# Delta rule of a hybrid decoder layer: per-head scalings and squares as ScalarE activations, the decay's subtraction as the exponential's bias, z's product as one VectorE instruction

## The chip, the cores and the metric

The kernel runs on one core of a Trainium2 chip. A core has five engines with queues of their own: PE (TensorE, matmuls), DVE (VectorE), ACT (ScalarE), POOL (GpSimd) and SP (SyncE, which here only issues DMAs). Each engine takes its instructions strictly in the order of the built program; semaphores hold an instruction until what it needs is there. The metric is the device time of one execution in microseconds; three runs of the kernel before gave 1560.11 to 1562.34 us, median 1561.56 us.

## The reference, cut to what matters

One decoder layer over 1024 tokens of width 1024, all in float32: RMSNorm, one input projection, then two groups of heads side by side, an output projection, a SwiGLU FFN, a gated embedding and a last norm. The change touches the gated delta rule of four heads (width 128, chunks of tokens; the kernel works with chunks of 128), and there these parts:

```python
gc = cumsum(g)                                   # per chunk, log decay
decay = where(lower, exp(gc[:, None] - gc[None, :]), 0)
kk = (k * beta) @ k.T * decay                    # strict lower part + identity = a_mat
u, w = solve(a_mat, [v * beta, k * beta * exp(gc)])
v_new = u - w @ state
o = (q * exp(gc)) @ state + (q @ k.T * decay) @ v_new
state = state * exp(g_last) + (k * exp(g_last - gc)).T @ v_new
o = o * rsqrt(mean(o * o) + EPS) * norm_w * silu(z)
```

## The kernel before, in words

The layer is one program in stages. First x is normalised and transposed and the v columns of the attention group are projected. Then comes the stage that matters here, from about 118 to 520 us: 24 units of the input projection ("pj": 128 output columns each, in two halves of 512 tokens, 24 matmuls of 128x512 per half) are the filling work of PE, and the delta rule of the four heads is woven between them. Softmax attention (from about 520 us), the FFN (from about 735 us) and the rest follow.

**Order of PE.** Generators (scan, prep, inv, output and so on) and the filler are woven by `weave` (L221). It asks a planner, class `Plan` (L53), when each operand will be ready. The planner adds fixed costs per instruction, by engine and free size (`op`, L94), and whenever no step of the delta rule is ready by its clock, one more group of three projection matmuls is put on PE. So PE's order is frozen while the program is written. The orders of ACT, DVE, POOL and, in this stage, SP come from a scheduler that runs afterwards on its own cost model. A change of instruction costs or engines therefore moves instructions on every engine.

**The delta rule, per head h and group g of four chunks.** `gates` (L512) makes the cumulative decays. `prep` (L703) transposes k and q, takes their norms, loads the row of decays (egb) by DMA and builds the decay matrix dt_ (subtraction with a per-partition scalar and a mask, four VectorE instructions of 128x128, then one Exp), multiplies it into the two products kk, and sends the triangular matrix nT to DRAM. `base` (L765) inverts small blocks with some 50 VectorE instructions and sends them through DRAM; it is tile names scr_pr, scr_uq, scr_ub. `inv` (L824) assembles the inverse U with PE (px, pz, pt, then pw, pu), ACT evacuating; X and ktok are k scaled per token, by GpSimd, after pz has read X's first content. `scan` (L899) is the serial recurrence over eight chunks (pr, pS, po). `emit_out` (L936) squares and sums the output o, scales it by its inverse norm, transposes it and multiplies by z. z itself is a projection unit: `z_half` (L609) evacuates it twice on ACT (plain, and tanh of half), GpSimd forms (1 + tanh) times plain in two instructions, and SP stores it.

The stretch from prep of a head to the end of its base is called a **base stretch** below, the stretch from there to the first step of the scan an **inversion stretch**. prep of head h+1 starts only after base of head h, and base of h+1 after inv of h, so these stretches follow each other for the four heads.

**Projection banks.** In this stage a projection half waits for one of two PSUM banks (`mmt`, L280); a bank is free when ACT has evacuated the half before the last (`conv_half` L580 into xb_g, `z_half`, or f_half).

Of the kernel before, what the change touches and what calls it, by code (L numbers as in the profile page):

```python
# [8 lines left out]
F32 = mybir.dt.float32  # L9
# [10 lines left out]
P = 128  # L20
# [167 lines left out]
def hybrid_layer(ctx, tc, x, p, attn_norm_w, w_in, conv_w, a_log, dt_bias, gdn_norm_w, fox_f_bias,  # L188
# [10 lines left out]
    def bc(ap, n):  # L199
        return ap.unsqueeze(len(ap.shape)).to_broadcast(list(ap.shape) + [n])  # L200
# [289 lines left out]
    def g4(tag, name, bufs=1, dt=F32, pool=None):  # L490
        pool = pool or (gpb if tag in ("scr", "nT", "X") else gp)
        return pool.tile([P, 4, P], dt, tag=tag, name=f"{tag}_{name}", bufs=bufs)
# [14 lines left out]
    egl = const.tile([P, NT, GH], F32, name="egl")  # L507
    egt = const.tile([P, NT, GH], F32, name="egt")
    kdw = const.tile([P, NT, GH], F32, name="kdw")
    beta = const.tile([P, NT, GH], F32, name="beta")  # L510

    def gates():  # L512
# [30 lines left out]
        mm(gl[:, 0:32], tri, ggf)  # L543
        mm(gl[:, 32:64], ones, ggf)
        V.tensor_copy(gcf, gl[:, 0:32])
        V.tensor_tensor(kdwf, gl[:, 32:64], gcf, op=ALU.subtract)
        A.activation(eglf, gl[:, 32:64], AF.Exp)
        A.activation(kdwf, kdwf, AF.Exp)
# [60 lines left out]
    def z_half(h, hf, ps):  # L609
        st = f(st1.tile([P, HALF], F32R, tag="fsh", name=f"zst{h}{hf}"))  # L610
        sp = f(st1.tile([P, HALF], F32R, tag="fsl", name=f"zsp{h}{hf}"))
        A.activation(sp, ps, AF.Copy)
        A.activation(st, ps, AF.Tanh, scale=0.5)
        G.tensor_tensor(st, st, sp, op=ALU.mult)
        G.tensor_tensor(st, st, sp, op=ALU.add)
        SY.dma_start(zs_d[h, :, hf * HALF:(hf + 1) * HALF], st)
        z_done[h] += 1

# [84 lines left out]
    def prep(h, g):  # L703
# [30 lines left out]
                                  ap=[[0, P], [GH * P, 4], [1, P]]))  # L734
        yield from ready(egb)
        dt_ = g4("scr", f"dt{nm}", 4)
        for j in range(4):
            V.scalar_tensor_tensor(dt_[:, j, :], egb[:, j, :], gc[:, t0 + j, h:h + 1], mbias,
                                   op0=ALU.subtract, op1=ALU.add)
        A.activation(egb, egb, AF.Exp)  # L740
        A.activation(dt_, dt_, AF.Exp)
        yield from ready(sm, dt_, slots=[SA])
        nT = nTs[h, g] = g4("nT", nm, 4)
        qkT = qkTs[h, g] = g4("qkT", nm, 2 * home(h)[1], pool=home(h)[0])
# [79 lines left out]
    def inv(h, g):  # L824
        nm = f"{h}_{g}"
        nT = nTs[h, g]
        kq, vT = kqv[h]
        tsl = slice(4 * g, 4 * g + 4)
        ktok, sm = ktoks[h, g], sms[h, g]
        U = g4("U", nm, 2)  # L830
        SY.dma_start(U, img(u_d[h], g))
        yield from ready(U)
        T = g4("X", f"T{nm}", 4)
        V.transpose(T.rearrange("p a b -> p (a b)"), U.rearrange("p a b -> p (a b)"))
        yield from ready(T, nT, slots=[SA])
        px = gpt(f"px5_{nm}")
        for j in range(4):
            mm(px[:, j, :], nT[:, j, :], T[:, j, :])
        X = g4("X", f"X{nm}", 4)
        A.activation(X, px, AF.Copy)  # L840
        yield from ready(X, slots=[SA])
        pz = gpt(f"pz5_{nm}")
        for j in range(4):
            mm(pz[:, j, :], X[:, j, :], U[:, j, :])
        V.copy_predicated(U, mask.unsqueeze(1).to_broadcast([P, 4, P]), pz)
        G.tensor_tensor(X, ktok, bc(egt[:, tsl, h], P), op=ALU.mult)
        G.tensor_tensor(ktok, ktok, bc(sm[:, 3], P), op=ALU.mult)
        yield from ready(U, slots=[SA])
        lo, hi = slice(0, 64), slice(64, P)
        pt = gpt(f"pt6_{nm}")  # L850
        for j in range(4):
            tr(pt[lo, j, lo], U[lo, j, lo], ident[lo, lo])
        A.activation(T[lo, :, lo], pt[lo, :, lo], AF.Copy)
        yield from ready(T, slots=[SA])
        px = gpt(f"px6_{nm}")
        for j in range(4):
            mm(px[hi, j, lo], nT[lo, j, hi], T[lo, j, lo])
        A.activation(T[hi, :, lo], px[hi, :, lo], AF.Copy)
        yield from ready(T, slots=[SA])
        pz = gpt(f"pz6_{nm}")  # L860
        for j in range(4):
            mm(pz[lo, j, hi], T[hi, j, lo], U[hi, j, hi])
        V.tensor_copy(U[lo, :, hi], pz[lo, :, hi])
        yield from ready(U, X, slots=[SA])
        pw = gpt(f"pw_{nm}")
        for j in range(4):
            mm(pw[:, j, :], X[:, j, :], U[:, j, :])
        A.activation(kq[:, tsl, 0], pw, AF.Copy, scale=-1.0)
        pu = gpt(f"pu_{nm}")
        for j in range(4):  # L870
            mm(pu[:, j, :], U[:, j, :], vT[:, 4 * g + j, :])
        V.tensor_tensor(vT[:, tsl], pu, bc(sm[:, 0], P), op=ALU.mult)
        yield from ready(kq, vT)
        left[h] -= 1
# [61 lines left out]
    def emit_out(h, g, o, sm):  # L936
        nm = f"{h}_{g}"
        sq = g4("osc", f"sqo{nm}", 2)
        G.tensor_tensor(sq, o, o, op=ALU.mult)
        so = small.tile([P, 4], F32, tag="so", name=f"so{nm}")  # L940
        V.tensor_reduce(so, sq, axis=AX.X, op=ALU.add)
        V.tensor_tensor(so, so, sm[:, 4], op=ALU.mult)
        V.tensor_tensor(so, so, sm[:, 4], op=ALU.mult)
        V.tensor_scalar(so, so, 1.0 / P, EPS, op0=ALU.mult, op1=ALU.add)
        ro = rsqrt(small, so, 4, f"o{nm}")
        V.tensor_tensor(ro, ro, sm[:, 4], op=ALU.mult)
        G.tensor_tensor(o, o, bc(ro, P), op=ALU.mult)
        while z_done[h] <= g:
            yield 0.5
        zt = g4("osc", f"zt{nm}", 2)  # L950
# [801 lines left out]
```

## Time and profile before

| | |
|---|---|
| runs | 1560.11, 1561.56, 1562.34 us (median 1561.56) |
| profiled execution | 1558.22 us, its span on the core 1556.5 us |
| mean granted TensorE clock | 0.972 of full speed |
| PE busy | 1467.6 us (94%), 7258 matmuls |
| DVE busy | 963.7 us (62%), 1989 instructions |
| ACT busy | 584.8 us (38%), 1211 instructions |
| POOL busy | 443.3 us (28%), 392 instructions |

Busy times are sums over the span. A matmul's end is modelled, so the distance from one start to the next tells more than its length. "PEclk" is the granted clock, 1.00 being 2.4 GHz and 0.50 being 1.2 GHz; a value between is a mean over the stretch. In a row such as `X_X<-ktok,egt ... x8 | 9.7, 1217 | 31.1 <-PE pz L154 20.5` the engine was busy 9.7 us with eight instructions of 1217 ns on average and sat idle for 31.1 us ahead of them, 20.5 us of it until PE's pz. Every operation goes through one helper, so the line is always L154 and the tiles tell operations apart.

### The profile page before, as it was taken

How to read it: one execution, taken by the hardware profiler on the slowest of the kernel's cores; microseconds unless marked ns; L12 is line 12 of the kernel's file. 1: busy time of each engine (PE TensorE's matmuls, PEld its weight loads, DVE VectorE, ACT ScalarE, POOL GpSimd, SP SyncE). 2: the span in 40 equal slices, each digit the busy share in tenths (PEclk: the TensorE clock that was granted, in tenths of full speed). 3: DMA queues.
4: the chain of work that ended last, by engine and by line, in shares of the span. 5: the costliest groups of instructions: out<-in, count | busy, mean ns of one | idle time of the engine just before them, and what ended most of it. 6: DMA issues, size and time to landing. Idle time of an engine off the chain costs nothing.

```text
span 1556.5 us, 20281 instructions
## 1 busy us (share of the span) xinstructions
PE 1467.6 (94%) x7258; PEld 1212.5 (78%) x7258; DVE 963.7 (62%) x1989; ACT 584.8 (38%) x1211; POOL 443.3 (28%) x392
## 2 busy tenths in 40 slices
PE   7999797989999899999689999999998999999997
PEld 6987686868787678887568888888887788888886
DVE  6569878796743367758955555555555442426555
ACT  5354433342333567755523323332322220214322
POOL 3023244344553465644422222322220000000000
PEclk9999898999999989999889999999999999999999
DMA  7322323234457876654122222222224832312022
GB/s 222 127 75 62 83 55 91 75 88 118 122 159 224 259 190 162 174 162 157 41 82 81 82 81 82 81 81 82 82 68 146 298 102 73 119 34 84 31 99 85
DMA packets 189701, 175.93 MB, mean 113 GB/s; under 512 B 30864, under 2 KB 147136, under 8 KB 189600
## 3 DMA queue, kind: packets, MB, share of 16 engines
q1 hardware_dynamic: 189200, 174.06, 38.1%
q8 instruction: 57, 0.93, 0.3%
q0 software_dynamic: 400, 0.57, 0.2%
q14 instruction: 44, 0.36, 0.1%
HBM read 122.53 MB, written 52.07 MB: 112 GB/s over the span
## 4 chain that ended last, share of the span: by engine, by line
PE 66%; DVE 18%; DMA 7%; ACT 3%; issue 2%; SPq 2%; POOL 1%; ACTq 0%; DVEq 0%; POOLq 0%
PE dn L154 15%; PE gC L154 8%; PE gD L154 7%; PE gA L154 7%; PE ppg L154 6%; PE pj L154 5%; PE gB L154 4%; DVE scr_pr L154 3%; DVE y_g L154 3%; PE v L154 2%; PE wog L154 2%; SPq L154 2%; DVE scr_uq L154 2%; PE po L154 2%; PE lg L154 1%
## 5 line engine op out<-in xcount | busy, mean ns | idle before, releaser
L154 PE MATMUL pj<-xna,wh_u 128*128 128x512 f32 x384 | 161.1, 420 | 9.5 <-ACT xb_g L154 8.5
L154 PE MATMUL pj<-xna,wl_u 128*128 128x512 f32 x384 | 152.9, 398 | 0.0
L154 PE MATMUL pj<-xnb,wh_u 128*128 128x512 f32 x384 | 152.7, 398 | 0.0
L154 ACT ACTIVATE whP<-fraw 128x512 fp32r<-128x512 f32 x110 | 68.5, 629 | 203.6 <-issue 101.1
L154 DVE TENSOR_TENSOR hr<-hr,dn 128x512 f32<-128x512 f32 x64 | 43.9, 687 | 114.5 <-PE dn L154 114.2
L154 POOL TENSOR_TENSOR s<-fraw 128x512 f32<-128x512 f32 x22 | 29.0, 1317 | 290.6 <-DMA fraw<-in_w_gate_up_dram 289.3
L154 PE MATMUL gD<-hb_T,whP 128*128 128x512 f32 x352 | 111.2, 397 | 0.0
L154 PE MATMUL gA<-hb_B,whP 128*128 128x512 f32 x352 | 111.1, 397 | 0.0
L154 POOL TENSOR_TENSOR wl_u<-wr_u,wh_u 128x512 fp32r<-128x512 f32 x48 | 70.1, 1481 | 116.0 <-ACT wh_u L154 80.9
L154 DVE TENSOR_TENSOR wlP<-fraw,whP 128x512 fp32r<-128x512 f32 x110 | 78.8, 720 | 29.4 <-ACT whP L154 29.4
L154 DVE TENSOR_TENSOR wlP<-s,whP 128x512 fp32r<-128x512 f32 x44 | 49.1, 1119 | 75.1 <-ACT whP L154 75.1
L154 PEld LDWEIGHTS pj<-xna,wh_u 128*128 128x128 f32 x384 | 74.0, 193 | 25.2 <-ACT xb_g L154 10.0
L154 PE MATMUL dn<-dh,al 128*128 128x512 f32 x224 | 89.7, 400 | 2.7 <-DVE al L154 2.7
L154 POOL TENSOR_TENSOR p<-p,rc 128x384 f32<-128x384 f32 (+3 forms) x64 | 72.6, 1146 | 63.4 <-DVE rc L154 45.3
L154 PE MATMUL dn<-dh,ah 128*128 128x512 f32 x224 | 89.4, 399 | 1.3 <-ACT ah L154 1.3
L154 PE MATMUL dn<-dl,ah 128*128 128x512 f32 x224 | 89.4, 399 | 0.5 <-DVE dl L154 0.5
L154 PEld LDWEIGHTS pj<-xna,wl_u 128*128 128x128 f32 x384 | 73.7, 192 | 16.4
L154 PEld LDWEIGHTS pj<-xnb,wh_u 128*128 128x128 f32 x384 | 74.1, 193 | 12.7
L154 PE MATMUL ppg<-dhp,pn 128*128 128x512 f32 (+1 forms) x272 | 81.8, 382 | 0.0
L154 PE MATMUL dn<-dn,ah 128*128 128x512 f32 x256 | 79.4, 391 | 0.0
L154 PEld LDWEIGHTS gA<-hb_B,whP 128*128 128x128 f32 x352 | 66.7, 190 | 15.9
L154 PEld LDWEIGHTS gD<-hb_T,whP 128*128 128x128 f32 x352 | 66.8, 190 | 15.8
(326 smaller groups left out, 3781.9 us busy)
## 6 DMA issues: line engine op xcount, KB each, us to landing
fraw<-in_w_gate_up_dram SPq DMA_DIRECT2D x44, 512.0 KB, 4.3
wr_u<-in_w_in_dram SPq DMA_DIRECT2D x24, 512.0 KB, 4.0
hb<-qk_d SPq DMA_DIRECT2D x24, 512.0 KB, 8.5
act_d<-th SPq DMA_DIRECT2D x44, 256.0 KB, 3.6
draw<-in_w_down_dram SPq DMA_DIRECT2D x22, 512.0 KB, 4.7
ar<-act_d SPq DMA_DIRECT2D x24, 384.0 KB, 3.3
v_d<-vs SPq DMA_DIRECT2D x16, 256.0 KB, 3.7
qk_d<-fsh SPq DMA_DIRECT2D x16, 256.0 KB, 3.5
```

Of the source, the lines that this page charges most:

```text
L154: r = f(*a, **kw)
```

## The change

- In `gates` a negated copy ngc of the cumulative decays is made once.
- In `prep` the four subtractions per group become one VectorE addition of the mask (128x512), and the subtraction becomes the bias of Exp, which is now four activations of 128x128.
- In `inv` X and ktok are scaled by eight ACT activations of 128x128 with a scale per partition, in place of two GpSimd instructions of 128x512.
- In `emit_out` the squares and their sums are four ACT activations with an accumulator (GpSimd's product and VectorE's reduction go), and the scaling by the inverse norm is four ACT activations (GpSimd's product goes).
- In `z_half` one VectorE instruction on 128x512 replaces GpSimd's two.

There are eight groups (four heads, two groups each) and eight halves of z.

```diff
@@ -507,6 +507,7 @@
     egl = const.tile([P, NT, GH], F32, name="egl")
     egt = const.tile([P, NT, GH], F32, name="egt")
     kdw = const.tile([P, NT, GH], F32, name="kdw")
+    ngc = const.tile([P, NT, GH], F32, name="ngc")
     beta = const.tile([P, NT, GH], F32, name="beta")
 
     def gates():
@@ -543,6 +544,7 @@
         mm(gl[:, 0:32], tri, ggf)
         mm(gl[:, 32:64], ones, ggf)
         V.tensor_copy(gcf, gl[:, 0:32])
+        V.tensor_scalar(ngc.rearrange("p t h -> p (t h)"), gl[:, 0:32], -1.0, None, op0=ALU.mult)
         V.tensor_tensor(kdwf, gl[:, 32:64], gcf, op=ALU.subtract)
         A.activation(eglf, gl[:, 32:64], AF.Exp)
         A.activation(kdwf, kdwf, AF.Exp)
@@ -611,8 +613,7 @@
         sp = f(st1.tile([P, HALF], F32R, tag="fsl", name=f"zsp{h}{hf}"))
         A.activation(sp, ps, AF.Copy)
         A.activation(st, ps, AF.Tanh, scale=0.5)
-        G.tensor_tensor(st, st, sp, op=ALU.mult)
-        G.tensor_tensor(st, st, sp, op=ALU.add)
+        V.scalar_tensor_tensor(st, st, 1.0, sp, op0=ALU.add, op1=ALU.mult)
         SY.dma_start(zs_d[h, :, hf * HALF:(hf + 1) * HALF], st)
         z_done[h] += 1
 
@@ -734,11 +735,10 @@
                                   ap=[[0, P], [GH * P, 4], [1, P]]))
         yield from ready(egb)
         dt_ = g4("scr", f"dt{nm}", 4)
+        V.tensor_tensor(dt_, egb, mbias.unsqueeze(1).to_broadcast([P, 4, P]), op=ALU.add)
+        A.activation(egb, egb, AF.Exp)
         for j in range(4):
-            V.scalar_tensor_tensor(dt_[:, j, :], egb[:, j, :], gc[:, t0 + j, h:h + 1], mbias,
-                                   op0=ALU.subtract, op1=ALU.add)
-        A.activation(egb, egb, AF.Exp)
-        A.activation(dt_, dt_, AF.Exp)
+            A.activation(dt_[:, j, :], dt_[:, j, :], AF.Exp, bias=ngc[:, t0 + j, h:h + 1])
         yield from ready(sm, dt_, slots=[SA])
         nT = nTs[h, g] = g4("nT", nm, 4)
         qkT = qkTs[h, g] = g4("qkT", nm, 2 * home(h)[1], pool=home(h)[0])
@@ -843,8 +843,10 @@
         for j in range(4):
             mm(pz[:, j, :], X[:, j, :], U[:, j, :])
         V.copy_predicated(U, mask.unsqueeze(1).to_broadcast([P, 4, P]), pz)
-        G.tensor_tensor(X, ktok, bc(egt[:, tsl, h], P), op=ALU.mult)
-        G.tensor_tensor(ktok, ktok, bc(sm[:, 3], P), op=ALU.mult)
+        for j in range(4):
+            A.activation(X[:, j, :], ktok[:, j, :], AF.Copy, scale=egt[:, 4 * g + j, h:h + 1])
+        for j in range(4):
+            A.activation(ktok[:, j, :], ktok[:, j, :], AF.Copy, scale=sm[:, 3, j:j + 1])
         yield from ready(U, slots=[SA])
         lo, hi = slice(0, 64), slice(64, P)
         pt = gpt(f"pt6_{nm}")
@@ -936,15 +938,16 @@
     def emit_out(h, g, o, sm):
         nm = f"{h}_{g}"
         sq = g4("osc", f"sqo{nm}", 2)
-        G.tensor_tensor(sq, o, o, op=ALU.mult)
         so = small.tile([P, 4], F32, tag="so", name=f"so{nm}")
-        V.tensor_reduce(so, sq, axis=AX.X, op=ALU.add)
+        for j in range(4):
+            A.activation(sq[:, j, :], o[:, j, :], AF.Square, accum_out=so[:, j:j + 1])
         V.tensor_tensor(so, so, sm[:, 4], op=ALU.mult)
         V.tensor_tensor(so, so, sm[:, 4], op=ALU.mult)
         V.tensor_scalar(so, so, 1.0 / P, EPS, op0=ALU.mult, op1=ALU.add)
         ro = rsqrt(small, so, 4, f"o{nm}")
         V.tensor_tensor(ro, ro, sm[:, 4], op=ALU.mult)
-        G.tensor_tensor(o, o, bc(ro, P), op=ALU.mult)
+        for j in range(4):
+            A.activation(o[:, j, :], o[:, j, :], AF.Copy, scale=ro[:, j:j + 1])
         while z_done[h] <= g:
             yield 0.5
         zt = g4("osc", f"zt{nm}", 2)
```

**What moves.** Number of projection matmuls that stand on PE between milestones of the delta rule (tv: last step of prep's matmuls; px5: first step of inv; pS: first step of the scan; numbers are head_group):

| stretch on PE | kind | before | now |
|---|---|---|---|
| tv_0_1 to px5_0_0 | base, head 0 | 189 | 168 |
| px5_0_0 to pS of head 0 | inversion, head 0 | 33 | 75 |
| pS of head 0 to px5_1_0 | base, head 1 | 141 | 117 |
| px5_1_0 to pS of head 1 | inversion, head 1 | 12 | 42 |
| pS of head 1 to px5_2_0 | base, head 2 | 189 | 159 |
| px5_2_0 to pS of head 2 | inversion, head 2 | 30 | 48 |
| pS of head 2 to px5_3_0 | base, head 3 | 126 | 126 |
| px5_3_0 to pS of head 3 | inversion, head 3 | 45 | 63 |

PE, start of the inversion of head 0. Before:

```order
L154 MATMUL px5_0_0_2024<-X_T0_0_1971,nT_0_0_1462 128x128 x4
L154 MATMUL px5_0_1_2031<-X_T0_1_1976,nT_0_1_1540 128x128 x4
L154 MATMUL kk0_1_0_2040<-kq1_1367 128x256 x2
L154 MATMUL pj8_1_2004<-xna1_107,wh_u8_1764 128x512
L154 MATMUL pj8_1_2004<-xnb1_109,wh_u8_1764 128x512
L154 MATMUL pj8_1_2004<-xna1_107,wl_u8_1765 128x512
L154 MATMUL pz5_0_0_2050<-U_0_0_1800,X_X0_0_2029 128x128 x4
```

Now:

```order
L154 MATMUL pj8_1_2004<-xna1_107,wh_u8_1764 128x512
L154 MATMUL pj8_1_2004<-xnb1_109,wh_u8_1764 128x512
L154 MATMUL pj8_1_2004<-xna1_107,wl_u8_1765 128x512
L154 MATMUL pz5_0_0_2031<-U_0_0_1806,X_X0_0_1992 128x128 x4
L154 MATMUL pj8_1_2004<-xna1_107,wh_u8_1764 128x512
L154 MATMUL pj8_1_2004<-xnb1_109,wh_u8_1764 128x512
L154 MATMUL pj8_1_2004<-xna1_107,wl_u8_1765 128x512
L154 MATMUL px5_0_1_2048<-X_T0_1_1982,nT_0_1_1551 128x128 x4
```

Both groups' px5 and pz5 stood next to each other with three projection matmuls between px5 and pz5; now the groups are apart, twelve projection matmuls stand between px5_0_0 and pz5_0_0, and group 1 comes later.

ACT, the same place (X_X: X of a group; xb_g12 is the PSUM evacuation and the tanh of a projection unit; X_T: steps of the inverse). Before:

```order
L154 ACTIVATE X_X0_0_2029<-px5_0_0_2024 128x512
L154 ACTIVATE X_X0_1_2036<-px5_0_1_2031 128x512
L154 ACTIVATE xb_g12_1994<-y_g12_1995 128x512
L154 ACTIVATE wh_u10_2103<-wr_u10_2101 128x512 x2
L154 ACTIVATE xb_g12_1994<-pj8_1_2004 128x512
L154 ACTIVATE X_T0_0_1971<-pt6_0_0_2082 64x4x64
L154 ACTIVATE X_T0_1_1976<-pt6_0_1_2088 64x4x64
L154 ACTIVATE y_g12_1995<-xb_g12_1994,cw_915 128x512
L154 ACTIVATE X_T0_0_1971<-px6_0_0_2116 64x4x64
L154 ACTIVATE X_T0_1_1976<-px6_0_1_2122 64x4x64
```

Now, from the third row behind the same first one:

```order
L154 ACTIVATE xb_g02_1818<-y_g02_1819 128x512
L154 ACTIVATE X_X0_0_1992<-ktok_0_0_1306,egt_970 128x128 x4
L154 ACTIVATE ktok_0_0_1306<-ktok_0_0_1306,sm0_0_1341 128x128 x2
L154 ACTIVATE y_g12_1995<-xb_g12_1994,cw_915 128x512
L154 ACTIVATE ktok_0_0_1306<-ktok_0_0_1306,sm0_0_1341 128x128 x2
L154 ACTIVATE X_X0_1_2053<-px5_0_1_2048 128x512
L154 ACTIVATE wh_u10_2073<-wr_u10_2071 128x512 x2
L154 ACTIVATE xb_g12_1994<-pj8_1_2004 128x512
L154 ACTIVATE X_T0_0_1975<-pt6_0_0_2083 64x4x64
L154 ACTIVATE xb_g12_1994<-y_g12_1995 128x512
L154 ACTIVATE y_g12_1995<-xb_g12_1994,cw_915 128x512
L154 ACTIVATE X_T0_0_1975<-px6_0_0_2095 64x4x64
```

The scalings of X and ktok now stand between the projection's evacuations and the steps of the inverse (X_T), on the queue that PE waits for at both.

DVE, base of head 0, where its last products begin. Before:

```order
L154 TENSOR_REDUCE scr_ub0_1572<-scr_pr0_1573 128x8x8
L154 COPY scr_uq0_1574<-scr_ub0_1572 32x4x16 x4
L154 TENSOR_TENSOR scr_pr0_1573<-scr_uq0_1574,nb0_1567 128x512
L154 TENSOR_REDUCE scr_uq0_1574<-scr_pr0_1573 128x2x16
L154 TENSOR_TENSOR scr_pr0_1573<-scr_uq0_1574,nb0_1567 128x512
```

Now:

```order
L154 TENSOR_REDUCE scr_ub0_1599<-scr_pr0_1600 128x8x8
L154 SCALAR_TENSOR_TENSOR zst00_1725<-zst00_1725,zsp00_1726 128x512
L154 COPY scr_uq0_1601<-scr_ub0_1599 32x4x16 x4
L154 SCALAR_TENSOR_TENSOR zst01_1756<-zst01_1756,zsp01_1757 128x512
L154 TENSOR_TENSOR scr_pr0_1600<-scr_uq0_1601,nb0_1594 128x512
L154 TENSOR_REDUCE scr_uq0_1601<-scr_pr0_1600 128x2x16
```

z's products of head 0 now stand inside base; the store of the second one stands, on SP, ahead of the load of unit 9's weights, which stood ahead of it before.

## Rows read from the trace of the kernel before

**Rows 1.** Windows view: stretch, length, busy per engine (count), PEclk, DMA share.

```profile
core 0: us, PE busy (x) PEld busy (x) DVE busy (x) ACT busy (x) POOL busy (x), PEclk, DMA share, GB/s
118.00:410.00 292.00, 259.41 (x1357) 215.39 (x1356) 245.69 (x576) 106.70 (x284) 118.86 (x101) 0.94 0.31 82
...
620.00:1557.00 937.00, 902.37 (x4079) 735.58 (x4078) 531.24 (x947) 309.73 (x532) 194.43 (x151) 0.98 0.33 101
...
118.00:520.00 402.00, 367.32 (x1958) 304.65 (x1956) 289.26 (x690) 151.38 (x380) 166.14 (x145) 0.96 0.40 112
```

**Rows 2.** Waits view, TensorE, 118 to 410 us: total, times, longest.

```profile
PE pS_s L154 <- DVE vT L154: 9.6, 4, 4.7
PE pj L154 <- ACT xb_g L154: 8.5, 3, 6.8
PE pr_s L154 <- DVE Ss L154: 8.3, 6, 2.5
PE px L154 <- ACT scr_dt L154: 3.1, 1, 3.1
PE pz L154 <- ACT X_X L154: 2.0, 1, 2.0
```

**Rows 3.** Timeline, TensorE: start, length, operation, idle time before it, releaser.

```profile
176.75 0.39 PE L154 MATMUL pj<-xnb,wh_u 128*128 128x512 f32 x1
176.97 0.39 PE L154 MATMUL pj<-xna,wl_u 128*128 128x512 f32 x1
184.19 0.80 PE L154 MATMUL pj<-xna,wh_u 128*128 128x512 f32 x1 [6.82 <-ACT xb_g L154]
184.78 0.63 PE L154 MATMUL pj<-xnb,wh_u 128*128 128x512 f32 x1
185.20 0.63 PE L154 MATMUL pj<-xna,wl_u 128*128 128x512 f32 x1
```

**Rows 4.** Groups by line, VectorE, 100 to 520 us: busy us, mean ns.

```profile
L154 DVE SCALAR_TENSOR_TENSOR y_g<-xb_g,cw,y_g 128x512 f32<-128x512 f32 x63 | 56.3, 893 | 5.1 <-ACT y_g L154 4.6
...
L154 DVE SCALAR_TENSOR_TENSOR scr_dt<-scr_egb,gc,mbias 128x128 f32<-128x128 f32 x32 | 15.0, 512 | 5.1 <-DMA scr_egb<-gc_d 5.1
...
L154 DVE SCALAR_TENSOR_TENSOR t_kq<-t_kq,ssq 128x8 f32<-128x8 f32 x24 | 6.5, 276 | 0.4
...
L154 DVE TENSOR_REDUCE so<-osc_sqo 128x4 f32<-128x512 f32 x8 | 5.5, 682 | 5.7 <-POOL osc_sqo L154 5.7
```

**Rows 5.** Tile views, y_g and t_kq: shortest, median, longest in ns.

```profile
L154 DVE SCALAR_TENSOR_TENSOR y_g<-xb_g,cw,y_g x72: 732/752/1797, 83.4 to 335.1; 128x512 f32<-128x512 f32 x72
...
L154 DVE SCALAR_TENSOR_TENSOR t_kq<-t_kq,ssq x24: 151/166/1259, 116.6 to 351.5; 128x8 f32<-128x8 f32 x24
```

**Rows 6.** Groups by line, GpSimd, 118 to 520 us.

```profile
L154 POOL TENSOR_TENSOR zst<-zst,zsp 128x512 f32<-128x512 f32 x16 | 24.8, 1547 | 11.2 <-ACT zst L154 10.7
...
L154 POOL TENSOR_TENSOR X_X<-ktok,egt 128x512 f32<-128x512 f32 x8 | 9.7, 1217 | 31.1 <-PE pz L154 20.5 <-ACT X_X L154 10.7
L154 POOL TENSOR_TENSOR osc_sqo<-oo_os 128x512 f32<-128x512 f32 x8 | 8.8, 1097 | 6.3 <-ACT oo_os L154 5.4 <-DVE osc_sqo L154 0.9
L154 POOL TENSOR_TENSOR ktok<-ktok,sm 128x512 f32<-128x512 f32 x8 | 8.7, 1092 | 0.2
L154 POOL TENSOR_TENSOR oo_os<-oo_os,y_o 128x512 f32<-128x512 f32 x8 | 8.4, 1052 | 29.7 <-DVE y_o L154 13.9 <-issue 7.9 <-PE pj L154 7.9
```

**Rows 7.** Groups by line, ScalarE, whole run.

```profile
L154 ACT ACTIVATE wh_u<-wr_u 128x512 fp32r<-128x512 f32 x48 | 27.7, 628 | 27.2 <-PE pj L154 21.6 <-DMA wr_u<-in_w_in_dram 5.6
...
L154 ACT ACTIVATE y_g<-xb_g,cw 128x512 f32<-128x512 f32 x24 | 17.3, 720 | 3.1 <-DVE kq L154 1.5 <-DVE t_kq L154 0.8
L154 ACT ACTIVATE scr_sq<-tk 128x128 f32<-128x128 f32 x64 | 16.8, 296 | 3.3 <-issue 3.1 <-PE tk L154 0.2
...
L154 ACT ACTIVATION_READ_ACCUMULATOR scr_sq<-tk 128x1 f32 x64 | 14.4, 230 | 0.0
...
L154 ACT ACTIVATE oo_os<-po_s 128x128 f32<-128x128 f32 x32 | 8.8, 276 | 44.7 <-PE po_s L154 44.5
```

## The prediction, made before the changed kernel was run

> **What bounds the kernel now.** I read the stretches first. From 620 us on PE is busy for 902 of 937 us, and nothing that the change edits runs there; from 118 to 410 us PE is busy for only 259.4 of 292 us, at a granted clock of 0.94, while DVE is busy for 245.7 us, 84% [rows 1]. So 32.6 us are idle in the stretch where the delta rule runs, and this is what the change can win or lose. Next, who ends the waits there: five rows hold 31.5 us, 17.9 us released by DVE (vT, Ss) and 13.6 us by ACT (xb_g, scr_dt, X_X) [rows 2]. The reader should see that a wait is a plan that was missed: PE's order is frozen, the planner puts projection matmuls where it thinks that DVE and ACT need time, and PE stands where they need more. The timeline shows the largest case: the next projection half starts 6.8 us late, and behind the wait matmuls start every 0.42 us in place of 0.22, at the lower of the two clock levels, 1.2 in place of 2.4 GHz [rows 3]. About twelve of them cost 2.4 us more, so I count each microsecond of idle time as 1.3.
>
> I split the waits by the two kinds of stretch that the order shows. The inversion stretches hold pz's 2.0 us (head 0) and the longest of pS, 4.7 us (head 2), 6.7 us together; the base stretches hold the other 24.8 us.
>
> **The change, part by part.** *VectorE's own work.* Removed: 32 subtractions (15.0 us) and eight reductions (5.5 us) [rows 4]. Added: eight mask additions and eight z products, all 128x512 with two SBUF inputs; the nearest row is y_g, the same form, at 893 ns, so 14.3 us. Net 6.2 us less. The one small instruction for ngc costs at most the 0.28 us of t_kq and lies before this stretch.
>
> *VectorE's waits for GpSimd.* y_g has a median of 752 ns but a mean of 893, and a t_kq of 128x8 takes 166 ns in the median and 1259 at worst, as long as a GpSimd product [rows 4 to 6]. 63 times 141 ns are 8.9 us; t_kq loses 24 times 110 ns, 2.6 us, and four more groups of 24 in the same Newton steps (y_kq, t_o and the products beside them) about as much each, so some 21 us are seen. GpSimd loses 60.4 of its 166.1 us [rows 1, 6], 36%. That share of 21 us is 7.6 us, the lower end. The upper end is that every removed microsecond was blocking DVE, 60.4 us. I take 14 us: near the lower end, since the projection's splits remain on GpSimd, but twice it, since the 128x512 products and the copies of base are not in the 21 us. VectorE then has 20 us less, 5 us per head, nearly all of it in the base stretches.
>
> *ScalarE.* 96 scalings and 32 exponentials of 128x128 with a scale or bias per partition: no such row exists. The lower end is 276 ns (copy from PSUM without it), the upper end 720 ns (the 128x512 form with it). I take 276 plus the 92 ns by which the operand lengthens the 128x512 form (720 against 628), 0.37 us, since the free size sets most of the difference [rows 7]. That is 47 us, less eight exponentials of 128x512 at 0.63 (5 us), plus 32 squares with accumulator at 0.296 + 0.230 us, 17 us: ACT goes from 151 to 210 of 402 us [rows 1, 7]. It stays half idle, so its sum costs nothing; its place in the chain does. Per head 16 scalings, 5.9 us, stand in ACT's queue among the steps of the inverse; half of them lie behind other waits (for pz, for px), so I charge 3 us per inversion, with ends 0 and 11.5 us.
>
> Here a rule speaks against the change. Four copies of 128x128 take 1.1 us and one of 128x512 0.63 us [rows 7]. The Trainium skill, VectorE: DVE Perf Modes, section "The TRN2 errata", says that instructions with SBUF sources pay a fixed latency each, that small tiles pay it every time, and advises tiles of at least 512 elements. The row agrees on the price; the rule does not ask whether anybody waits. If the cut tiles lay wholly on the path, 5.9 us per inversion, the sum below would give 1559 us in place of 1546.
>
> *GpSimd and SP.* GpSimd's cut is worth nothing by itself, it is idle for more than half of the stretch. On SP the load of unit 9's weights now stands behind z's second store, which waits for a product inside base: up to two products, 1.8 us, covered by the projection half (5.4 us) that is still to run. Were that cover gone, PE would pay those 1.8 us.
>
> *PE's order.* The planner priced the new instructions too. By the table of the order, the base stretches now hold 75 projection matmuls fewer, 17.0 us at 0.227 us each, and the inversions 108 more, 24.5 us. So in the base stretches PE arrives earlier and gives up most of what VectorE wins, and in the inversions it has far more cover than ScalarE costs.
>
> **The sum.** Inversions: head 0 has 2.0 - 9.5 + 3 = -4.5 us, head 1 0 - 6.8 + 3 = -3.8, head 2 4.7 - 4.1 + 3 = 3.6, head 3 0 - 4.1 + 3 = -1.1. A 3.6 us wait is left, and the 8.3 us of spare time of heads 0 and 1 let VectorE get ahead before the base stretch that follows. Base: 24.8 + 17.0 - 20 - 8.3 = 13.5 us, plus 2 us since the last base stretch has only some 3 us of waits to lose: 15.5. Together 19.1 us in place of 31.5, 12.4 us less, 16 us with the clock. The profiled execution took 1558.2 us, 3.3 us under the median of the runs; 1542 for it is 1545.5 for the median, and I predict **1546 us**. Outside this stretch some rows swap places and I charge nothing. What is late next is base of head 0, whose block inversion on VectorE is longer than the plan allows, as before.
>
> **The rivals.** *ScalarE's queue takes over the waits (slower).* GpSimd stood 13.9 us for y_o and 20.5 us for pz [rows 6], and nothing hung on it. Now ACT stands there, and behind it in its queue are the evacuations that free PE's two banks, as well as the steps of the inverse. Against it: over eight instructions each these are 1.7 and 2.6 us, and PE has 5.4 us in hand, a half of 24 matmuls; it decides from the point where ACT's wait and the work behind it exceed this. For it: xb_g is already where PE waits 8.5 us [rows 2]. If 20 of the 34.4 us reach PE, the idle time is 39.1 us, 7.6 more than now: 10 us with the clock, 1571.
>
> *The plan gives it all back (same).* The cut tiles lie on the path, as in the paragraph on the rule: inversions -1.6, 0, 6.5 and 1.8 us, base 24.8 + 17.0 - 20 - 1.6 + 2 = 22.2, together 30.5 us, 1 us less than now. With the 17 us that the plan moved out of the base stretches nothing is left: 1560 us, or 1559 with what rounding hides. For it: the plan shortens the base stretches by nearly as much as VectorE wins.
>
> *VectorE is freed more (much faster).* If GpSimd's removed time had mostly blocked VectorE, its 60.4 us plus 6.2 empty the base stretches: only 3.6 us of waits remain, 27.9 us less, 36 with the clock: 1525. Against it: y_g's median is 20 ns above its shortest, so most instructions meet no GpSimd at all [rows 5].
>
> **How the numbers follow.** Forecast (1546, own range 1536 to 1555) 0.52; much faster (1525) 0.12; same (1560) 0.16; slower (1571) 0.20. A measurement of this kernel tells about 0.2%, 3 us, from no change. Faster is 0.52 + 0.12 = 0.64, same 0.16, slower 0.20. The range reaches from 1530, which leaves out half of the much faster case, to 1571, which leaves out half of the slower one; the ends of ScalarE's price and of VectorE's waits that lie beyond are left to these halves.
>
> **What would show it.** In the changed profile I expect PE's idle time from 118 to 410 us near 20 us with a clock above 0.94; waits on pz and on the second pS gone; DVE's busy time in the delta stage down by some 20 us, with y_g's mean nearer to its median; scalings on ACT at about 0.37 us; ACT some 60 us busier. I am wrong if PE's waits on ACT (xb_g, X_T, zsp) grow beyond the 13.6 us of now, if the scalings take over 0.5 us, or if y_g's mean does not move.

## The result and the profile after

The change took 1542.01 us (median of four runs, 1540.99 to 1545.1) against 1560.99 us before: ratio 0.9881, 95% interval 0.9864 to 0.9898. That is 19 us faster, and inside the predicted range of 1530 to 1571 us. The profiled execution of the change has a span of 1543.4 us.

The windows view of the change over the stretches of [rows 1] (same columns):

```profile
118.00:410.00 292.00, 264.66 (x1412) 219.47 (x1411) 233.63 (x577) 140.89 (x423) 73.06 (x67) 0.97 0.34 90
...
118.00:520.00 402.00, 365.64 (x1968) 303.03 (x1966) 269.78 (x676) 196.45 (x567) 104.32 (x96) 0.97 0.41 115
```

VectorE has 19.5 us less in 402 us (289.3 to 269.8), ScalarE 45 us more. But PE still stands for 27.3 of the 292 us, where it stood for 32.6: only 5.3 us less. The waits view, TensorE, 118 to 410 us, answers to [rows 2]:

```profile
PE pS_s L154 <- DVE vT L154: 14.8, 7, 4.0
PE px L154 <- DVE ssq L154: 6.6, 1, 6.6
PE pr_s L154 <- DVE Ss L154: 5.6, 4, 2.5
PE px L154 <- ACT X_T L154: 0.3, 1, 0.3
```

The waits on ScalarE (xb_g, scr_dt, X_X) are gone, but VectorE's rows have grown from 17.9 to 27.0 us although VectorE does less. That cannot make 19 us. So I laid the milestones of PE of both traces beside each other (us from the span's start):

| | before | the change | difference |
|---|---|---|---|
| last projection matmul | 490.0 | 478.4 | -11.6 |
| first matmul of the FFN's gate (gA) | 740.8 | 738.2 | -2.6 |
| first matmul of the down projection (dn) | 1201.3 | 1194.1 | -7.2 |
| end of the span | 1556.5 | 1543.4 | -13.1 |

The delta rule's stage wins 11.6 us, attention gives 9.0 us back, and from the FFN on, where no instruction was edited, 10.5 us are won. In this last part the timelines of TensorE differ in one thing. Before, from 1000 us (start, length, operation, how many in the row):

```profile
1000.00 0.63 PE L154 MATMUL gC<-hb_B,whP 128*128 128x512 f32 x2
...
1002.80 0.39 PE L154 MATMUL gD<-hb_T,whP 128*128 128x512 f32 x1
```

The change, the same stretch:

```profile
1000.13 0.62 PE L154 MATMUL gD<-hb_T,whP 128*128 128x512 f32 x2
...
1002.85 0.39 PE L154 MATMUL gA<-hb_B,whP 128*128 128x512 f32 x1
```

From the first start shown to the last, twelve matmuls take 2.80 us before (233 ns each) and 2.72 us after (227 ns), with nobody waiting and a granted clock of 0.99 from 800 to 1100 us in both. Some 3,300 matmuls of 128x512 lie in this part; they start every 232 ns on average before and every 227 after, which is 16 us. The one thing there that I could see the change to alter is where tiles lie: the new tile ngc has 128 bytes per partition and moves everything allocated behind it on the left side of SBUF. In the built program before, the FFN's tiles on the left side (ah, and part of whP and of hb) start at 96 modulo 256, those on the right side (dh, dl, and the rest of whP and hb) at 224, and some 2,600 of these matmuls read one operand from each kind; in the change all of these tiles start at 224. A contrast inside one profile says the same. In the groups by line, TensorE, 800 to 1460 us, before, the first row's operands lie on different sides, the second's both on the left:

```profile
L154 PE MATMUL dn<-dh,ah 128*128 128x512 f32 x224 | 89.4, 399 | 1.3 <-ACT ah L154 1.3
L154 PE MATMUL dn<-dn,ah 128*128 128x512 f32 x256 | 79.4, 391 | 0.0
```

In the change they are 392 and 390 ns. So three effects were to be told apart: the addresses, PE's new order (the planner's prices), and the instructions on the other engines.

### The profile page after: what moved, and what is told of

The parts are those of the page before. It is cut to its first block, busy times and chain, and to the rows that moved or that the text cites. A ratio compares the mean times of both kernels' runs of the same rounds, so it can differ in the third digit from the quotient of the medians.

```text
span 1543.4 us, 20339 instructions
## 1 busy us (share of the span) xinstructions
PE 1443.4 (94%) x7258; PEld 1203.9 (78%) x7258; DVE 943.0 (61%) x1966; ACT 628.8 (41%) x1395; POOL 381.7 (25%) x344
## 4 chain that ended last, share of the span: by engine, by line
PE 64%; DVE 15%; DMA 9%; ACT 5%; issue 3%; SPq 2%; POOL 1%; ACTq 0%; DVEq 0%; POOLq 0%
PE dn L154 15%; PE gC L154 7%; PE gA L154 7%; PE gD L154 7%; PE pj L154 7%; PE ppg L154 6%; PE gB L154 4%; DVE scr_pr L154 3%; DMA woraw<-in_w_out_dram 3%; PE v L154 2%; DVE y_g L154 2%; DVE scr_uq L154 2%; SPq L154 2%; ACT p L154 1%; DMA nb<-n_d 1%
## 5 line engine op out<-in xcount | busy, mean ns | idle before, releaser
L154 PEld LDWEIGHTS pj<-xna,wh_u 128*128 128x128 f32 x384 | 73.5, 191 | 16.1 <-issue 2.4
L154 PEld LDWEIGHTS pj<-xnb,wh_u 128*128 128x128 f32 x384 | 73.6, 192 | 12.3
L154 ACT ACTIVATE ah<-ar 128x768 fp32r<-128x768 f32 (+1 forms) x32 | 25.2, 791 | 128.9 <-PE dn L154 127.3
```

The costliest lines, as they stand in the source:

```text
L154: r = f(*a, **kw)
```

## The experiments

All times are medians; the kernel before ran beside each batch with 1560.8 to 1561.9 us.

### Addresses, order and instructions apart

**The kernel before with the address shift alone (before_shift128).** No other tile, no instruction and no order differs.

```diff
     kdw = const.tile([P, NT, GH], F32, name="kdw")
+    ngc = const.tile([P, NT, GH], F32, name="ngc")
```

> The kernel before with the 128-byte tile ngc allocated in the same place as the change has it, never written or read; every instruction and every order is that of before, only the addresses behind it move by 128 bytes. Theory S (shift): the change moves the left side of SBUF by 128 bytes, so that a matmul's two operands, which lay 128 bytes apart modulo 256 where one is on the left and one on the right side, now agree; in the profile of before matmuls of the FFN start every 232 ns, in that of the change every 227. From the first gate matmul to the end PE was busy 784.6 us before and 767.0 after, and that stretch took 815.7 and 805.2 us. So 10 to 18 us of the 19 us measured come from the address alone: this kernel takes 1543 to 1551 us, its matmuls of the FFN start every 227 ns, and its stretch from 118 us to the last projection matmul stays at 372 us. Theory D (delta rule, my prediction): the whole gain comes from shorter waits in the delta rule; this kernel takes 1561 us, as before.

Measured: 1545.28 us (six runs), ratio 0.9906, interval 0.9889 to 0.9923: 15.5 us faster, with every instruction and its order those of before. Twelve matmuls from 1000.18 to 1002.90 us, 227 ns each, and the pair of rows above is now

```profile
L154 PE MATMUL dn<-dh,ah 128*128 128x512 f32 x224 | 87.9, 392 | 2.0 <-ACT ah L154 1.4 <-ACT dh L154 0.7
L154 PE MATMUL dn<-dn,ah 128*128 128x512 f32 x256 | 79.1, 390 | 0.0
```

From the first gate matmul to the end it takes 798.4 us in place of 815.7. The last projection matmul came at 494.9 us, 4.9 later than before, which I did not expect and did not follow up; it came at 494.8 us in before_shift64 below, so any shift may cost this stage some 5 us. That stays open. Theory S stands: four fifths of the 19 us come from an unread tile.

**The change without the shift (after_noshift).**

```diff
-    ngc = const.tile([P, NT, GH], F32, name="ngc")
+    ngc = gg
```

> The changed kernel with ngc kept in the storage of gg, which is dead by then, so that all addresses are those of before; the order is that of the change but for 9 rows on ScalarE. Theory S: the matmul spacing of the FFN is back at 232 ns and the kernel takes 10 to 18 us more than the change, 1552 to 1560 us; what is left under 1561 us is what the new instructions and the new order win together. Theory D: 1542 us, as the change.

Measured: 1558.74 us (twelve runs), ratio 0.9991, interval 0.998 to 1.0002. What the change does to engines and order is worth 2.1 us together, not told from nothing.

**New instructions, old order (new_ops_old_prices).** At each edited place the planner is charged for the old instruction, then the new one is issued; for example

```diff
+        plan.price("G", X, ktok, bc(egt[:, tsl, h], P))
+        plan.price("G", ktok, ktok, bc(sm[:, 3], P))
         for j in range(4):
             A.activation(X[:, j, :], ktok[:, j, :], AF.Copy, scale=egt[:, 4 * g + j, h:h + 1])
```

> The changed kernel, but the planner is charged for the instructions of before: PE's order is row for row that of before, the instructions on the other engines are those of the change, the addresses too. By my prediction the base stretches then lose nearly all of their 24.8 us of waits, since PE no longer arrives 17 us earlier, and the inversion stretches keep theirs, 2.0 + 0 + 4.7 + 0 us, with 3 us each for ScalarE, so about 19 us of idle in place of 33: within 3 us of the change. Rival O (order): what helps in the delta rule is the 108 projection matmuls moved into the inversions, so without them the stretch from 118 us to the last projection matmul takes over 366 us (360 in the change, 372 before) and the kernel is 5 us or more slower than the change. Rival E (engines): the new order does harm, and this kernel is 5 us or more faster than the change.

Measured: 1529.34 us, ratio 0.9802, interval 0.9785 to 0.9819: 12.7 us faster than the change. Rival E.

**Old instructions, new order (old_ops_new_prices).** The reverse: the old instructions, the planner charged for the new.

> The instructions of before with the addresses of the change, but the planner is charged for the change's instructions: PE's order is row for row that of the change, VectorE, GpSimd and ScalarE do the old work. By my prediction PE arrives 17 us earlier in base stretches that are as long as before: base waits of 24.8 + 17 = 42 us, inversions none, so 10 us more of idle than before and 13 us with the clock: 13 us slower than before_shift128. Rival O (order): the new order alone brings the delta rule's gain, and the stretch from 118 us to the last projection matmul takes 362 us or less.

Measured: 1566.40 us, ratio 1.0041, interval 1.0027 to 1.0056: 21.1 us slower than before_shift128, where I had expected 13.

All four have the addresses of the change:

| | order of before | order of the change |
|---|---|---|
| instructions of before | 1545.3 | 1566.4 |
| instructions of the change | 1529.3 | 1542.0 |

The instructions win 16.0 us under the old order (24.4 under the new), and the order costs 12.7 us (21.1 with the old instructions). The profile of new instructions with the old order, windows, the same stretches, and its waits from 118 to 490 us:

```profile
118.00:410.00 292.00, 270.23 (x1464) 224.83 (x1463) 232.00 (x583) 146.28 (x439) 74.89 (x66) 0.97 0.34 90
...
118.00:520.00 402.00, 373.51 (x2039) 309.88 (x2038) 275.08 (x693) 203.92 (x587) 114.79 (x104) 0.98 0.44 123
```

```profile
PE pr_s L161 <- DVE Ss L161: 7.5, 6, 2.2
PE pS_s L161 <- DVE vT L161: 7.3, 5, 2.8
PE pj L161 <- ACT xb_g L161: 3.9, 1, 3.9
PE pz L161 <- ACT X_X L161: 1.7, 2, 1.4
```

VectorE's and ScalarE's busy times are within 6 and 8 us of the change's, yet PE is idle for 21.8 us where it was for 27.3. The 6.6 us before px (the end of base of head 0) is gone, since PE has more projection matmuls there, and pS_s is halved.

**Where the new order loses.** Milestones of the kernels with the shift:

| us | before_shift128 | new_ops_old_prices | the change |
|---|---|---|---|
| first step of the scan, head 0 | 218.6 | 210.6 | 218.0 |
| last pS_s of the scan | 469.0 | 449.1 | 462.8 |
| last projection matmul | 494.9 | 475.0 | 478.4 |
| first gate matmul | 743.0 | 727.8 | 738.2 |
| end of the span | 1541.4 | 1528.9 | 1543.4 |

Against the same instructions in the old order the change ends its projection 3.4 us later, needs 7.0 us more for attention and 4.1 us more from there on (the change's profiled execution lies some 3 us above its median, so that a part of this is scatter; and in the new order a last transposition, tp_n, stands behind the gate's first three matmuls and not ahead of them, so that some 2 us of the 4.1 still belong to attention). The new order delays the delta rule: with the projection matmuls that it puts there, the inversion of head 0 (first px to first pS) takes 35.8 us, 25.7 with the old order, and the recurrence behind it ends 15.6 us before the projection does, 26 us with the old order. The same holds for all four heads. Lengths of the base stretches (from 118 us) and of the inversion stretches, each summed over the heads, and the start of head 3's scan, in us:

| | base stretches | inversion stretches | first step of the scan, head 3 |
|---|---|---|---|
| before_shift128 | 220.1 | 107.2 | 445.5 |
| old_ops_new_prices | 214.0 | 130.2 | 462.1 |
| new_ops_old_prices | 206.6 | 101.5 | 426.1 |
| the change | 205.5 | 117.6 | 441.1 |

With the old instructions the new order shortens the base stretches by 6.1 us and lengthens the inversions by 23.0; with the new ones by 1.1 and 16.1 us. The scan of the last head starts 16.6 and 15.0 us later by it, and the kernel takes 21.1 and 12.7 us longer: a projection matmul that covers a wait in an inversion also delays the inversion's own next step, and the heads follow each other.

The recurrence's last output then collides with attention's start. The waits and windows of the first 250 us behind the projection, the change, then old order:

```profile
PE lg L154 <- ACT p L154: 7.0, 4, 4.8
PE pp L154 <- ACT pst L154: 5.7, 1, 5.7
PE pT L154 <- DVE ptl L154: 4.9, 7, 2.0
...
481.20:738.20 257.00, 236.00 (x1376) 199.12 (x1375) 159.92 (x352) 153.47 (x350) 133.54 (x129) 0.97 0.66 183
```

```profile
PE lg L161 <- ACT p L161: 3.6, 3, 2.0
...
PE pp L161 <- ACT pst L161: 1.2, 1, 1.2
...
477.30:727.80 250.50, 235.20 (x1372) 197.77 (x1371) 162.77 (x364) 154.23 (x353) 134.72 (x130) 0.97 0.68 184
```

The chain of the change from 474 to 553 us shows what the 5.7 us wait for: a store of 9 us that starts only behind the delta rule's last output (start, us, what):

```profile
478.83 3.34 DMA osc_zt<-zs_d
...
482.30 0.76 DVE osc_zt L154
...
485.44 9.26 DMA pp_d<-pst
494.73 0.04 ACTq L154
```

That this collision is the whole of the 7.0 us is argued, not shown.

**Do better prices make a better order? (measured_prices).** The change, its planner charged what the trace shows:

```diff
+            if name == "activation" and hasattr(kw.get("scale"), "tensor") and n == P:
+                dur = 0.39
+            if name == "activation" and hasattr(kw.get("bias"), "tensor") and n == P:
+                dur = 0.41
+            if name == "activation" and "accum_out" in kw and n == P:
+                dur = 0.49
             end = self.take(e, r, dur)
```

> The changed kernel, where the planner charges ScalarE's instructions of 128x128 with a scale or bias per partition or with an accumulator what the trace shows (0.39, 0.41 and 0.49 us in place of 0.20, 0.20 and 0.29). Theory U (the change's new order is bad because its prices are too low: the planner believes that four copies take 0.8 us, they take 1.56): PE arrives later, waits less, and the kernel comes near the one with the order of before, 1529 to 1535 us. Rival L (any new order is a draw: the order of before had been fitted to this kernel's waits, and prices do not tell what is right): within 4 us of 1542 us, or slower.

Measured: 1562.09 us (twelve runs), ratio 1.0005, interval 0.9992 to 1.0017: 20 us slower than the change. Theory U is wrong; the "or slower" of Rival L holds. With dearer instructions the planner puts projection matmuls in earlier and has none left: the projection ends at 469.5 us, the recurrence at 508.2, 39 us behind it, and attention, as I read the waits, has nothing to fill PE with. Waits, TensorE, 118 to 760 us:

```profile
PE lg L160 <- ACT p L160: 16.4, 6, 6.2
PE pr_s L160 <- DVE Ss L160: 15.2, 9, 2.8
PE pz L160 <- ACT X_X L160: 6.2, 1, 6.2
```

### Which addresses

**Shift by 64 bytes (before_shift64).** As before_shift128, with a tile of 16 floats.

> The kernel before, its left side moved by 64 bytes in place of 128. If a matmul is slow wherever its two operands differ modulo 256, the FFN's matmuls start every 230 us/1000 or more as in before, 232 ns on average, and the kernel takes 1556 us or more. If only a distance of 128 is slow, or any move helps, they start every 227 ns and it takes 1545 us.

Measured: 1558.93 us, one run. Twelve matmuls of the gate take from 999.84 to 1002.60 us, 230 ns each; over the FFN they start every 231 ns on average, 232 in before and 227 in before_shift128, and from the first gate matmul to the end it takes 810.8 us, 815.7 and 798.4 in these two. Operands 64 bytes apart are nearly as slow as 128 bytes apart; those of the projection and the FFN that agree modulo 256 (both at 96 or both at 224) run at 227 ns. That the distance modulo 256 decides is read from these distances alone, and it is not the whole: the matmuls of attention's output projection (wog), with both operands at 224, start every 230 to 231 ns in before, in both shifted kernels, in after_noshift and in the change. What in the reads behind it conflicts is open. The Trainium skill, SBUF — State Buffer, section "Who interferes with whom", gives PE two read ports, one for the moving operand and one for the weights, "independent"; these runs show a cost of 3 to 6 ns per matmul that depends on where the two lie to each other.

### The parts of the change

These start from new_ops_old_prices (1529.3 us) and put one part back; PE's order stays that of before, row for row.

**The decay put back (op_undo_dt):** four `V.scalar_tensor_tensor` and one Exp.

> The kernel with the change's instructions and before's PE order (1529 us), with only the decay put back: four VectorE subtractions of 128x128 and one Exp of 128x512. Theory V (each part is worth what it takes from VectorE, its own instructions and the products of GpSimd that blocked it): 15.0 us of subtractions against 5.5 us of mask additions, 9.5 us of the 20 that VectorE lost, so 7 us slower, 1536 us. Rival P (one part does it all: the decay stands at the head of every base stretch): 16 us slower, 1545 us.

Measured: 1531.50 us, ratio 0.9809 (0.9784 to 0.9834): 2 us, not told from nothing, where Theory V wanted 7 and Rival P 16.

**z's product put back (op_undo_z):**

```diff
-        V.scalar_tensor_tensor(st, st, 1.0, sp, op0=ALU.add, op1=ALU.mult)
+        G.tensor_tensor(st, st, sp, op=ALU.mult)
+        G.tensor_tensor(st, st, sp, op=ALU.add)
```

> The same kernel with only z's product put back on GpSimd, two products per half. Theory V: VectorE loses 6.4 us of its own products and gets back some 6 us of blocking by 24.8 us of GpSimd products, so nothing: 1528 to 1531 us. Rival G (the gain is GpSimd's time as such, since 24.8 of the 60.4 us removed are these): 6 us or more slower, 1535 us. Rival P: 1529 us.

Measured: 1541.60 us, ratio 0.9875 (0.9854 to 0.9896): 12.3 us slower. Rival G, and by twice its bound; Theory V is wrong on this part. The windows up to the last projection matmul, with z on VectorE and with z on GpSimd:

```profile
118.00:475.00 357.00, 334.23 (x1821) 278.35 (x1821) 257.64 (x653) 177.93 (x527) 98.12 (x84) 0.98 0.38 106
```

```profile
118.00:487.60 369.60, 336.43 (x1821) 280.25 (x1819) 270.40 (x644) 178.42 (x527) 121.26 (x100) 0.97 0.37 103
```

VectorE loses eight products (6.2 us) and is busy for 12.8 us more: 19 us of blocking by 24.0 us of GpSimd products, nearly four fifths. The timelines of op_undo_z, GpSimd and then VectorE, show how:

```profile
340.99 2.54 POOL L161 TENSOR_TENSOR wl_u<-wr_u,wh_u 128x512 fp32r<-128x512 f32 x2 [6.20 <-ACT wh_u L161]
343.48 2.62 POOL L161 TENSOR_TENSOR zst<-zst,zsp 128x512 f32<-128x512 f32 x2
```

```profile
342.34 1.21 DVE L161 TENSOR_TENSOR t_kq<-y_kq 128x8 f32<-128x8 f32 x1
343.59 1.19 DVE L161 SCALAR_TENSOR_TENSOR t_kq<-t_kq,ssq 128x8 f32<-128x8 f32 x1
344.81 0.17 DVE L161 SCALAR_TENSOR_TENSOR y_kq<-t_kq,y_kq 128x8 f32<-128x8 f32 x1
345.01 1.11 DVE L161 TENSOR_TENSOR sm<-beta,y_kq 128x4 f32<-128x4 f32 x1
346.04 0.15 DVE L161 TENSOR_TENSOR sm<-ssq,y_kq 128x4 f32<-128x4 f32 x1
```

Instructions of four and eight columns that take 0.15 to 0.17 us alone take 1.1 to 1.2 us, and each of the three ends where a GpSimd product ends (343.5, 344.8, 346.1); the first of these products is a split of the weights, which both kernels have, the other two are z's. z's products come in the middle of base and prep, where VectorE is the bound, and as two in a row. The Trainium skill, SBUF — State Buffer, section "Who interferes with whom", has this rule: a VectorE instruction with two SBUF inputs contends with a GpSimd instruction that reads SBUF, and whoever holds the shared pair holds it for the whole instruction. The trace agrees, and gives the price here: 0.8 us of VectorE for each microsecond of z's products.

The largest single loss is in copies of base that read a single tile. The groups by line, VectorE, 118 to 520 us, with z on VectorE and then on GpSimd:

```profile
L161 DVE COPY scr_uq<-scr_ub 32x64 f32<-32x64 f32 x16 | 2.9, 184 | 0.2
```

```profile
L161 DVE COPY scr_uq<-scr_ub 32x64 f32<-32x64 f32 x16 | 6.5, 409 | 0.2
```

A rival is left: z's products could also hurt by filling GpSimd's own queue. The waits of TensorE in op_undo_z, 118 to 490 us, speak against it, and the timeline of ScalarE tells what the longest of the third row stands for:

```profile
PE pS_s L161 <- DVE vT L161: 11.3, 5, 4.2
PE pr_s L161 <- DVE Ss L161: 9.6, 6, 4.1
PE pj L161 <- ACT xb_g L161: 7.1, 2, 6.8
```

```profile
178.65 0.63 ACT L161 ACTIVATE xb_g<-y_g 128x512 f32<-128x512 f32 x1 [12.03 <-DVE y_g L161]
```

PE waits for no GpSimd instruction there, in neither kernel. Its waits on VectorE's vT and Ss grow from 14.8 to 20.9 us, those on xb_g from 3.9 to 7.1, and ahead of the longest of these ScalarE itself had stood 12 us for VectorE.

**The scalings of X and ktok put back (op_undo_Xk).**

> The same kernel with only the scalings of X and ktok put back on GpSimd, 2 products per group in place of eight ScalarE copies. Theory V: 18.4 us of GpSimd come back, some 4 us of blocking: 3 us slower, 1532 us. My prediction charged the copies 3 us per inversion, 12 us in all; if that holds, undoing them gains: 1525 us or less. Rival P: 1529 us.

Measured: 1528.52 us, ratio 0.9795 (0.9771 to 0.982): no difference, where Theory V wanted 3 us more and my prediction's charge 4 us less. Neither GpSimd's 18.4 us nor ScalarE's 64 copies matter here.

**The output's squares and scaling put back (op_undo_out).**

> The same kernel with only the output's squares, sum and scaling put back on GpSimd and VectorE. Theory V: 5.5 us of reductions and some 4 us of blocking by 17.2 us of GpSimd products come back, partly in stretches where VectorE is ahead: 5 us slower, 1534 us. Rival P: 1529 us.

Measured: 1527.16 us, ratio 0.978 (0.9758 to 0.9802): 2 us faster with the old form, not told from nothing, where Theory V wanted 5 us more.

**z's product alone (op_z_only):** everything else as before.

> The instructions of before with before's PE order and the addresses of the change, and of the change only z's product as one VectorE instruction (ngc is written and not read). Theory Z (z's product is the whole gain of the engines, because its 24.8 us of GpSimd products blocked VectorE): 12 us under before_shift128, 1533 us. Rival A (each part takes away some blocking; undoing the others singly cost nothing only because the rest was still gone): less than half of it, 1539 us or more.

Measured: 1532.11 us, ratio 0.9813 (0.9789 to 0.9837): 13.2 us under before_shift128. Theory Z: one instruction in place of two brings the gain of the engines by itself.

**z's product and the decay (op_z_dt).**

> The same with the change's decay as well (mask addition and four Exp with a bias); scalings and squares stay on GpSimd and VectorE. Adding up from the single undo runs (out 2.2 and X with ktok 0.8 us faster when undone): 1526 us. Adding up from below (z 12.3, decay 2.2 us under before_shift128): 1531 us. Rival A: over 1535 us.

Measured: 1525.42 us (six runs), ratio 0.977 (0.9743 to 0.9796): beside the old scalings the decay is worth 6.7 us, though the two intervals overlap at their ends. The sum from the undo runs, 1526 us, fits. By its median it is the fastest of all (op_undo_out, 1.7 us behind, cannot be told from it), 16.6 us under the change and 35 under the kernel before. It has two of the four parts, the address shift, and the order of PE of before.

## Why the prediction was right, and where it was wrong

The time came out as forecast, 1542 against 1546 us, but by another sum, so that the number is luck. The change's engines and order are worth 2.1 us without the shift (after_noshift, 1558.7 us): this was the rival "the plan gives it all back", 1560 us, which I gave 0.16. The other 16.7 us (from after_noshift to the change) came from addresses, of which the prediction says nothing.

- **VectorE's own work and its waits for GpSimd: right.** I took 20 us off VectorE; 19.5 us are gone. Its own instructions lost 8.6 us (I had 6.2; the new ones are cheaper than the 893 ns of y_g), the rest I read as blocking. The groups by line, VectorE, 100 to 520 us, of the change:

```profile
L154 DVE SCALAR_TENSOR_TENSOR y_g<-xb_g,cw,y_g 128x512 f32<-128x512 f32 x63 | 53.7, 853 | 8.3 <-ACT y_g L154 7.5
...
L154 DVE SCALAR_TENSOR_TENSOR zst<-zst,zsp 128x512 f32<-128x512 f32 x8 | 6.4, 804 | 0.0
...
L154 DVE TENSOR_TENSOR scr_dt<-scr_egb,mbias 128x512 f32<-128x512 f32 x8 | 5.5, 692 | 5.6 <-DMA scr_egb<-gc_d 3.0 <-ACT scr_sq L154 1.8 <-issue 0.7
...
L154 DVE SCALAR_TENSOR_TENSOR t_kq<-t_kq,ssq 128x8 f32<-128x8 f32 x24 | 4.9, 207 | 0.4
```

- **What it is worth: the size was met by chance.** The forecast of 16 us was for instructions and order together; 16.0 us is what the instructions win where PE's order is kept, and with the new order 3.3 us of it are left (before_shift128 to the change). That GpSimd's blocking was the lever was right too, but I spread it over all 60.4 us of GpSimd's products; nearly all of it hung on z's.
- **ScalarE's price: right; its place on the path: wrong.** I took 0.37 us for a 128x128 with a scale or bias. My row for four small copies (1.1 us, against 0.63 for one large one) reads from PSUM; from SBUF the four take 1.56 us, so that the price is higher still. The groups by line, ScalarE, up to 520 us, show

```profile
L154 ACT ACTIVATE ktok<-ktok,sm 128x128 f32<-128x128 f32 x32 | 11.5, 389 | 0.0
L154 ACT ACTIVATE X_X<-ktok,egt 128x128 f32<-128x128 f32 x32 | 10.9, 390 | 3.7 <-PE pz L154 3.6
L154 ACT ACTIVATE scr_dt<-scr_dt,ngc 128x128 f32<-128x128 f32 x32 | 10.4, 407 | 0.0
...
L154 ACT ACTIVATE osc_sqo<-oo_os 128x128 f32<-128x128 f32 x32 | 9.7, 304 | 4.5 <-DVE osc_sqo L154 4.1
...
L154 ACT ACTIVATION_READ_ACCUMULATOR osc_sqo<-oo_os 128x1 f32 x32 | 6.0, 188 | 0.0
```

  The 3 us per inversion that I charged are not there: with the old order the inversion of head 0 (px to the first pS) takes 25.7 us, 28.7 in before_shift128, and op_undo_Xk costs and wins nothing. So the rule on small tiles, by which 1559 us would have come out, did not decide here: ScalarE had the time. The rival that its queue takes over the waits did not happen either; ScalarE's rows fell.
- **PE's order: the step that failed.** I let the plan take back 17.0 us in the base stretches and give cover for 24.5 in the inversions, as if cover cost nothing, and credited the base stretches with 8.3 us of it as time for VectorE to get ahead. In the change the inversions hold 0.3 us of waits, where the sum had 3.6, so the cover is real; but the base stretches hold 27.0 us, where it had 15.5 (heads 0 to 3: 8.9, 8.3, 4.7 and 3.0 us before, 6.6, 5.3, 8.7 and 6.4 in the change). Without the credit the sum gives 23.8. And the cover is paid for in length: before, the base stretches take 218.1 us and the inversions 104.6; in the change 205.5 and 117.6, so that the scan of head 3 starts at 441.1 us in place of 440.7. The order by itself costs 12.7 us with the new instructions and 21.1 with the old. Matmuls put into an inversion stand before the recurrence, and its end comes later; the prediction looked at the idle time of one stage and not at when the recurrence ends.
- **"Outside this stretch I charge nothing": wrong.** The one new tile was priced by its instruction, 0.28 us; its 128 bytes were worth 15.5 us.
- **The signs named.** ScalarE's waits vanished, pz's among them, and so did the 4.7 us of pS in head 2's inversion; y_g's mean fell from 893 to 853 ns, its median stayed at 752; ScalarE is 45 us busier, not 60; the wait named as next, the end of base of head 0, came (6.6 us before px); idle time was 27.3 us, not 20; the clock 0.97.

## What to carry to other kernels

A new tile moves every tile behind it: when a stage that nobody edited gets faster or slower, compare the distance of matmul starts there, and run the old kernel with the tile allocated and unread. Where an order is frozen from a cost model, an edit of instructions is two edits: price the new instruction as the old one to keep the order, and judge the order by a run of its own; truer prices gave a worse one. Filling work that covers a wait on a serial chain also lengthens the chain: look at where the chain ends, and not only at the idle time. And what a GpSimd product costs is the VectorE instructions that it holds up where VectorE is the bound: one of four parts did nearly all of it.

## What the runs showed of the hardware that I had not expected

In the FFN a 128x512 float32 matmul starts every 227 ns where its two operands' addresses agree modulo 256, and every 230 to 233 where they lie 64 or 128 bytes apart: 15.5 us of 1561. z's GpSimd products take four fifths of their own time from VectorE where they fall into a stretch of its small instructions, those with two SBUF inputs and copies of one tile alike.
